# Score tiles as views of one three-bank PSUM tile, channel-major values, and a summed first projection, in a two-layer hybrid block

## The chip, the cores and the metric

The kernel runs on one core of one Trainium2 chip. The metric is the device time of one execution in microseconds (us); lower is better. PE is TensorE, DVE VectorE, ACT ScalarE, POOL GpSimd, SP SyncE; PSUM has eight banks of 512 fp32 columns on each of its 128 partitions.

## The reference

Two layers act on 512 image tokens and 256 context tokens of width 1024. Cut to what matters here:

```
for i in range(2):
    u = modulate(rmsnorm(h, norm1_g[i]), sh1, sc1) @ w_in[i]      # and the same for the context
    y_a = ssd_mixer(...);  y_b = diff_mixer(...);  y_c = gqa_mixer(...);  y_d = mla_mixer(...)
    h = h + g1 * (concat(y_a, y_b, y_c, y_d) @ w_out[i])
    h = h + g2 * (relu(modulate(rmsnorm(h, norm2_g[i]), sh2, sc2) @ mlp_w1[i])**2 @ mlp_w2[i])
return rmsnorm(h, final_norm_g)
```

`y_b` is a differential attention (two softmaxes for each of 4 heads), `y_c` and `y_d` are ordinary attentions of 4 heads each, `y_a` is a chunked state-space scan. Image queries attend to the 768 keys of image and context, context queries (layer 0 only) to the 256 context keys.

## The kernel before, in words

Activations lie channel-major, 8 tiles of 128 channels by 768 tokens (`XS` the 512 of the image, `CS` the 256 of the context). Every fp32 product is made from fp32r parts: a weight and an activation are each split in a high and a low part (`split`, L699), and three matmuls (high by high, high by low, low by high) are summed for each tile of the contraction (`gemm`, L726). One matmul has 512 columns for the image, and its partner 256 for the context.

`big_gemm` (L736) makes one output tile of 128 channels by 768 tokens (layer 1, which needs only the image: 512 or 256 tokens) in one PSUM tile from `ps_s` (L487), 48 matmuls in all, then hands it to an `evac`: in the MLP's first half ACT's relu (`up_jobs`, L1678, names `r<-p` in the profile), in its second half and in the output projection DVE's residual sums (`residual`, L1613, `h<-p`, `h<-pq`, `h<-pr`). `scores` (L1043) uses the same kind of PSUM tile for the 128 x 768 scores of one head and one block of queries; DVE takes their maximum (`maxed`, `d_m<-d_s`) and ACT their exponential (`exped`, `d_p<-d_s,d_m`). The probabilities are normalised, transposed on PE (`g_t<-ident,g_p`) and multiplied with the values. All other products, transposes and sums use PSUM tiles of one bank (`ps_t`, `ps_g`, ..., tag "g").

PSUM before: two tiles of 1024 columns (tag "S", two banks each) and four single banks.

The values of the differential attention and of the second attention (`dv`, `gv`) are made token-major by `v_start` and `v_step` (L872, L880): for each of 6 blocks of 128 tokens and each of 8 contraction tiles three matmuls of 384 columns. In layer 0 they are the first product: it runs contraction tile by contraction tile while the tiles `xn_0` to `xn_7` of the first norm become ready. `pdk` (first keys) follows.

The order of the work is not the order of the code. Every call on an engine is recorded by `Plan.take` (L217) with a cost from a small model; `Plan.order` (L245) then simulates the five engines and writes each engine's instructions in the order in which that simulation starts them; `Plan.issue` (L322) emits them in this one global order. All instructions of the profile therefore stand at the helper's line L331. The framework below adds the waits: it keeps a record for each PSUM or SBUF tile of who wrote and who read it last, in the order of emission. `Later` stands for a tile before its buffer is known.

Of the kernel before, what the change touches and what calls it, by code (L numbers as in the profile page):

```python
# [19 lines left out]
P = 128  # L20
# [17 lines left out]
def _r(c, n=P):  # L38
# [10 lines left out]
    "ckv": _r(C_CKV),  # L49
}  # L50
T_COLS = np.concatenate([_r(C_DV, 256), _r(C_GV)])
# [67 lines left out]
class Later:  # L119


    def __init__(self, pool, shape, dt, name, tag, bufs):
        self.args = (pool, shape, dt, name, tag, bufs)
        self.dt, self.tag, self.bufs = dt, tag, bufs
        self.made = None
        self.reads, self.writes = [], []
        self.left, self.end, self.first, self.last, self.kind, self.slot = 0, 0.0, None, None, None, None
        self.cols = int(np.prod(shape[1:]))
        self.base = np.empty(shape, np.int8)
        self.mem = self.base.__array_interface__["data"][0]  # L130

    def ap(self):
        pool, shape, dt, name, tag, bufs = self.args
        if self.made is None and bufs == 1:
            self.made = pool.tile(list(shape), dt, name=name, tag=tag, bufs=1)
# [15 lines left out]
class Pool:  # L151
# [3 lines left out]
    def tile(self, shape, dt, name, tag, bufs):  # L155
        t = Later(self.pool, shape, dt, name, tag, bufs)
        return View(t, (), t.base)


class Op:  # L160


    def __init__(self, n, eng):
        self.n, self.eng, self.calls, self.cost, self.late = n, eng, [], 0.0, 0.0
        self.before, self.after, self.tiles = set(), [], []
        self.start = self.end = 0.0


class Plan:
# [15 lines left out]
    def cost(self, eng, name, args, kw, out):  # L185
# [3 lines left out]
        if eng == "PE":  # L189
# [5 lines left out]
            m = w.width()  # L195
# [19 lines left out]
        return 0.45, 1.2  # L215

    def take(self, eng, fn, name, args, kw):  # L217
        out = kw["out"] if "out" in kw else args[0]
        writes = [x for x in (out, kw.get("accum_out")) if isinstance(x, View)]
# [8 lines left out]
        op.calls.append((fn, args, kw))  # L228
        op.cost += cost
# [15 lines left out]
    def order(self):  # L245
        tags = {}
        for op in self.ops:
            op.wait = len(op.before)
            op.rank = op.n - (self.EARLY if op.eng not in ("PE", "SP") and any(t.tag in ("S", "g") for t in op.tiles) else 0)
# [9 lines left out]
        ready = {e: [] for e in free}  # L259
        held = []  # L260
# [25 lines left out]
        while len(out) < len(self.ops):  # L286
            best = None
            for e, ops in ready.items():
                if not ops:
                    continue  # L290
# [6 lines left out]
            op = min((o for o in ready[e] if o.at <= s), key=lambda o: o.rank)  # L297
            ready[e].remove(op)
            cost = op.cost
# [6 lines left out]
            if e == "SP":  # L306
                dma = max(dma, op.end) + op.bytes / 250e3
# [14 lines left out]
    def issue(self):  # L322
        import os
        out = self.order()
        if os.environ.get("PLAN"):
            report(out)
# [47 lines left out]

def report(out):
    free, idle = {}, {}
    for op in out:
        e = op.eng
        w = int(op.start // 50)
        g = op.start - free.get(e, 0.0)  # L380
        idle.setdefault(e, {}).setdefault(w, 0.0)
        idle[e][w] += g
        free[e] = op.start + op.cost
    print("plan ends", max(o.end for o in out), {e: round(sum(o.cost for o in out if o.eng == e), 1) for e in free})
    for e in ("PE", "DVE", "ACT"):
        print(e, [round(idle[e].get(w, 0.0), 1) for w in range(40)])
# [46 lines left out]
def hybrid_block_kernel(ctx: ExitStack, tc: tile.TileContext, a: dict, out: bass.AP, dbg=None):  # L433
# [18 lines left out]
    NSC = 2  # L452
    GAP = 8
    UP_MODS = (1, 2, 3, 4)
    DN_MODS = ((1, 1, 2, 1, 2, 1, 2, 1), (1, 1, 2, 1, 2, 1, 2, 1), (1, 1, 2, 1, 2, 1, 2, 1), (2, 2, 2, 2, 2, 2, 2, 2))
    ORD0 = "gk ga gb cqx z0 xs0 xs1 cq0 b c z1 ckv".split()
    ORD1 = "gk ga gb z0 b xs1 cqx xs0 z1 c cq0 ckv".split()
# [28 lines left out]

    def ps_s(name):  # L487
        return pp.tile([P, 1024], F32, name=name, tag="S", bufs=2)

    def ps_t(name):  # L490
        return pp.tile([P, 512], F32, name=name, tag="g", bufs=4)

    def ps_v(name):
        return pp.tile([P, 512], F32, name=name, tag="g", bufs=4)

    def ps_o(name):
        return pp.tile([P, 512], F32, name=name, tag="g", bufs=4)

    def ps_g(name):
        return pp.tile([P, 512], F32, name=name, tag="g", bufs=4)  # L500

    def ps_r(name):
        return pp.tile([P, 512], F32, name=name, tag="g", bufs=4)
# [335 lines left out]
    def v_weights(l, q):  # L839
        return weights(f"wv{l}_{q}", a["wv"][l, :, q], 384, gtt if l == 0 else tt)  # L840

    wv = [v_weights(0, q) for q in range(4)]
    for i in range(3):
        mod_dma(i)
        next(wv[i])
# [9 lines left out]
    xn = [pair(f"xn0_{k}") for k in range(KT)]  # L855
    def xn_start(i):
# [10 lines left out]
        for k, t in late:  # L867
            for si, s in ((0, XS), (1, CS)):
                (LO0 if si in LOP else stt)(out=xn[k][1][:, s], in0=t[:, s], scalar=sh[:, k, si : si + 1], in1=f(xn[k][0][:, s]),
                    op0=ALU.add, op1=ALU.subtract)  # L870

    def v_start(l):  # L872

        lay[l].dv = [unit(f"dv{l}_{i}", (P, 3, 256)) for i in range(2)]
        lay[l].gv = unit(f"gv{l}", (P, 6, P))
        big = [ps_s(f"pv{l}_{i}") for i in range(2)]
        return [big[0][:, 0:384], big[0][:, 512:896], big[1][:, 0:384], big[1][:, 512:896],
                ps_t(f"pva{l}")[:, 0:384], ps_t(f"pvb{l}")[:, 0:384]]

    def v_step(l, vps, w, xn, k):  # L880
        for t in range(6):
            for wi, xi in ((0, 0), (1, 0), (0, 1)):
                mm(vps[t], xn[k][xi][:, P * t : P * t + P], w[k % 2][wi],
                   start=k == 0 and wi == 0 and xi == 0, stop=k == KT - 1 and xi == 1)
            yield 0.49
        if k == KT - 1:
            for t in range(6):
                act(lay[l].dv[t // 3][:, t % 3], vps[t][:, 0:256], AF.Copy)
                nc.vector.tensor_copy(lay[l].gv[:, t], vps[t][:, 256:384])

    def value_of(gen):
        while True:
            try:
                next(gen)
            except StopIteration as e:
                return e.value

    for i, s in enumerate((XS, CS)):
        run(rstd_of(f"n1_0_q{i}", psq[i], rb, s))
    ws = [value_of(wv[0])]  # L900
    mod_done(0, mod_load(0))
    xn_start(0)
    ws.append(value_of(wv[1]))
    m = mod_load(1)
    mod_dma(3)
    next(wv[3])
    vps = v_start(0)
    for q in range(4):
        run(v_step(0, vps, ws[q], xn, 2 * q))
        if q < 3:  # L910
            mod_done(q + 1, m)
            xn_start(q + 1)
        if q < 2:
            ws.append(value_of(wv[q + 2]))
        run(v_step(0, vps, ws[q], xn, 2 * q + 1))
        if q < 2:
            m = mod_load(q + 2)
# [58 lines left out]
    def mixers(l, xn, yd, h, ys):  # L976
# [7 lines left out]
        raw = {}  # L984
        done = set()
# [13 lines left out]
        def proj(name, toks, evac, how, after=None):  # L999
            def use(w):  # L1000
                yield from how(f"p{name}{l}", w, xn, toks, evac, len(TILES[name]))
# [4 lines left out]
        def v_jobs():  # L1006
            vps = []

            def use(w, q):
                if q == 0:  # L1010
                    flush()
                    vps.extend(v_start(l))
                for k in (2 * q, 2 * q + 1):
                    yield from v_step(l, vps, w, xn, k)

            return [(lambda q=q: v_weights(l, q), lambda w, q=q: use(w, q)) for q in range(4)]
# [26 lines left out]
        def scores(name, passes, t):  # L1043
# [68 lines left out]
        def diff_attn(j):  # L1112
# [24 lines left out]
            def vcols(hh, kt):  # L1137
                return L.dv[kt // 3][:, kt % 3, 64 * (2 * j + hh) : 64 * (2 * j + hh) + 64]
# [16 lines left out]
        def plain_attn(name, j, jobs, vcols, kout, flag, s_cost):  # L1155
            while flag not in done:
# [258 lines left out]
        def silu_z(name):  # L1415
            def evac(ps, s):
                if name not in raw:
                    raw[name] = unit(f"sz{name}{l}")
                t = sc(f"zt{name}{l}_{s.start}", s.stop - s.start)
                ts(t, ps, -80.0, None, op0=ALU.max)  # L1420
                sigmoid_of(t)
                tt(out=raw[name][:, s], in0=ps, in1=t, op=ALU.mult)
# [102 lines left out]
        def ready(j):  # L1525
            if ("dk", j, 1, 1) in dst and ("dq", j, 1, 1) in dst:
                done.add(("d", j))

        def dproj(n, how):
            toks = BOTH if n[:2] == "dk" else QT  # L1530

            def after():
                yield from diff_prep(n[:2], int(n[2]))
                yield K.hop_d
                ready(int(n[2]))

            return proj(n, toks, keep(n, 1.0 if n[:2] == "dk" else 32.0 ** -0.5), how, after)
# [9 lines left out]
        def gproj(n, how=side_gemm):  # L1547
            toks = BOTH if n in ("cqx", "b", "xs0", "xs1", "gk", "ckv") else QT
# [4 lines left out]
                     "c": setter("ssd"), "z1": setter("z"), "ckv": setter("mla")}.get(n)  # L1553
# [284 lines left out]
```

## Time and profile before

| | us |
|---|---|
| median of 3 runs (lowest to highest) | 1814.16 (1813.57 to 1814.26) |
| the profiled execution's own time | 1812.9 |
| its span in the profile | 1811.2 |
| PE busy in the span | 1732.4 |
| DVE, ACT, POOL busy | 1085.0, 875.6, 469.4 |

The profile shows one execution. Busy time is the time in which an engine has an instruction in work; "idle before" in a group is the time in which the engine had nothing before an instruction of that group, and the arrow names what ended it. PEclk is the share of full speed that was granted to TensorE. A name as `p<-a_0h,w_0s` is output from inputs; the digits of layers and buffers are left out. In time, layer 0's mixers and attention take some 25 to 425 us, its output projection and MLP 425 to 1075, layer 1's mixers 1075 to 1475, and its output projection and MLP the rest.

### The profile page before, as it was taken

To read this page: it belongs to the slowest core of one execution; us is meant where nothing else is said; L and a number is where in the kernel's file an instruction comes from. 1 tells how busy PE (TensorE), PEld (TensorE's weight loads), DVE (VectorE), ACT (ScalarE), POOL (GpSimd) and SP (SyncE) were. 2 spreads that over 40 slices of the span, in tenths; PEclk is the share of its full clock that TensorE was granted. 3 is DMA by queue.
4 is the path that set the end of the run, shared out by engine and by line. 5 is a ranking of instruction groups with operands and counts; after the bars stand their busy time and mean duration, and the time that the engine had idled before them with its cause. 6 is when DMAs were issued, how large, how long until landed. Compare 5 with 4: busy or idle time off the path is not lost. (4 is left out here: it accounts for less than half of the span.)

```text
span 1811.2 us, 30203 instructions
## 1 busy us (share of the span) xinstructions
PE 1732.4 (96%) x11206; PEld 1464.8 (81%) x11206; DVE 1085.0 (60%) x2112; ACT 875.6 (48%) x1776; POOL 469.4 (26%) x437
## 2 busy tenths in 40 slices
PE   6999999899999999999999999999799999999997
PEld 4878787677878888888888888887678998888886
DVE  4476968787584864543544184887886873333324
ACT  4355767687455223123122353777676762323243
POOL 2322342120244002001002664335110320101056
PEclk9999999999999999999999999999899999999999
DMA  9375431024344543432433334422014552323333
GB/s 354 94 214 150 122 105 37 17 53 162 109 157 141 171 141 96 158 118 87 156 123 99 133 107 133 127 77 59 12 49 152 172 177 93 97 95 94 97 110 126
DMA packets 117330, 216.28 MB, mean 119 GB/s; under 512 B 15424, under 2 KB 24640, under 8 KB 117184
## 3 DMA queue, kind: packets, MB, share of 16 engines
q1 hardware_dynamic: 117184, 214.36, 38.1%
q8 instruction: 88, 1.44, 0.3%
q14 instruction: 58, 0.48, 0.1%
HBM read 185.99 MB, written 8.13 MB: 107 GB/s over the span
## 5 line engine op out<-in xcount | busy, mean ns | idle before, releaser
L331 ACT ACTIVATE w_0s<-w 128x512 fp32r<-128x512 f32 x256 | 160.9, 630 | 387.4 <-PE p L331 352.2
L331 POOL TENSOR_TENSOR r<-r 128x512 f32<-128x512 f32 (+2 forms) x80 | 92.5, 1156 | 652.1 <-ACT a_0h L331 387.4
L331 DVE TENSOR_TENSOR w_0s<-w,w_0s 128x512 fp32r<-128x512 f32 x216 | 149.9, 697 | 184.2 <-ACT w_0s L331 179.1
L331 DVE SCALAR_TENSOR_TENSOR h<-p,modT,h 128x512 f32<-128x512 f32 (+1 forms) x104 | 63.0, 625 | 140.4 <-PE p L331 140.4
L331 ACT ACTIVATE r<-p 128x512 f32<-128x512 f32 (+2 forms) x80 | 47.8, 597 | 166.6 <-PE p L331 165.2
L331 DVE SCALAR_TENSOR_TENSOR junk<-mv,cb 128x512 bf16<-128x512 f32 x128 | 90.2, 716 | 46.2 <-DMA mv<-in_modw_dram 45.4
L331 DVE TENSOR_REDUCE d_m<-d_s 128x1 f32<-128x768 f32 (+1 forms) x80 | 66.4, 846 | 34.8 <-PE d_s L331 33.9
L331 ACT ACTIVATE d_p<-d_s,d_m 128x768 f32<-128x768 f32 (+1 forms) x80 | 65.0, 816 | 37.0 <-DVE d_m L331 28.0
L331 POOL TENSOR_TENSOR w_0s<-w,w_0s 128x512 fp32r<-128x512 f32 x40 | 54.2, 1363 | 28.1 <-ACT w_0s L331 26.3
L331 POOL TENSOR_TENSOR acc<-acc,sq 128x256 f32<-128x256 f32 (+1 forms) x48 | 49.9, 1041 | 42.3 <-ACT sq L331 41.8
L331 PE MATMUL p<-xm_0h,w_0s 128*128 128x512 f32 (+1 forms) x176 | 54.7, 357 | 0.1
L331 PE MATMUL p<-xm_3h,w_0s 128*128 128x512 f32 (+1 forms) x176 | 54.5, 356 | 0.0
L331 PE MATMUL p<-a_0h,w_0s 128*128 128x512 f32 (+1 forms) x176 | 54.1, 354 | 0.3 <-POOL w_0s L331 0.2
L331 PE MATMUL p<-xm_7h,w_0s 128*128 128x512 f32 (+1 forms) x176 | 54.2, 354 | 0.0
L331 PE MATMUL p<-xm_4h,w_0s 128*128 128x512 f32 (+1 forms) x176 | 54.0, 353 | 0.0
L331 PE MATMUL p<-a_5h,w_0s 128*128 128x512 f32 (+1 forms) x176 | 54.0, 353 | 0.0
L331 PE MATMUL p<-a_3h,w_0s 128*128 128x512 f32 (+1 forms) x176 | 54.0, 353 | 0.0
L331 PE MATMUL p<-xm_6h,w_0s 128*128 128x512 f32 (+1 forms) x176 | 53.9, 353 | 0.0
L331 PE MATMUL p<-a_7h,w_0s 128*128 128x512 f32 (+1 forms) x176 | 53.8, 352 | 0.0
L331 PE MATMUL p<-xm_5h,w_0s 128*128 128x512 f32 (+1 forms) x176 | 53.8, 352 | 0.0
L331 PE MATMUL p<-xm_2h,w_0s 128*128 128x512 f32 (+1 forms) x176 | 53.8, 352 | 0.0
L331 PE MATMUL p<-a_4h,w_0s 128*128 128x512 f32 (+1 forms) x176 | 53.8, 352 | 0.0
(2346 smaller groups left out, 5552.6 us busy)
## 6 DMA issues: line engine op xcount, KB each, us to landing
w<-in_w_dram SPq DMA_DIRECT2D x320, 256.0 KB, 2.6
mv<-in_modw_dram SPq DMA_DIRECT2D x96, 256.0 KB, 2.7
mk<-in_modk_dram SPq DMA_DIRECT2D x64, 256.0 KB, 3.4
wr<-in_wout_dram SPq DMA_DIRECT2D x32, 256.0 KB, 2.7
h<-in_xT_dram SPq DMA_DIRECT2D x16, 384.0 KB, 7.6
mw<-in_mod_dram SPq DMA_DIRECT2D x16, 384.0 KB, 6.3
wo<-in_wout_dram SPq DMA_DIRECT2D x32, 192.0 KB, 2.4
wv<-in_wv_dram SPq DMA_DIRECT2D x16, 192.0 KB, 5.0
```

The source lines that it names most:

```text
L331: i = fn(*[x.real() if isinstance(x, View) else x for x in args], **{k: x.real() if isinstance(x, View) else x for k, x in kw.items()}).ins
```

## The change

1. `ps_s` no longer gives two tiles of two banks each. One tile `wide` of 1536 columns (three banks) is made once, and the two slots S0 and S1 are views of its columns 0 to 767 and 768 to 1535. Each slot has one bank of its own and half of the middle one. Since a matmul stays in one bank, `big_gemm` and `scores` cut slot S0 at column 512 and S1 at column 256. For views (`of`) no buffer dependency is added by hand.
2. The bank that becomes free goes to the general tiles: five instead of four.
3. The planner gets a rule (`barred`): a sum may not be opened in a shared bank while another slot has one open there.
4. `dv` and `gv` become ordinary channel-major projections (`dv0`, `dv1`, `gvv`) and are transposed on PE afterwards (`v_prep`: 18 transposes and 6 ACT copies for each layer, in place of 144 matmuls' token-major form and 12 copies).
5. In layer 0 four projections (`dk0`, `dq0`, `dv0`, `dk1`) are summed side by side, contraction tile by contraction tile, as the norm tiles come (`first_step`), where the values stood before.
6. The planner's model of DMAs changes (latency 1.2 to 1.4, 250 to 330 KB/us), and `silu_z` copies its PSUM tile to SBUF first.

The diff, cut to its core:

```diff
+    wide = pp.tile([P, 2 * NT], F32, name="wide", tag="wide", bufs=1)
+    turn = [0]
     def ps_s(name):
-        return pp.tile([P, 1024], F32, name=name, tag="S", bufs=2)
+        i = turn[0] = 1 - turn[0]
+        return pp.tile([P, NT], F32, name=name, tag=f"S{i}", bufs=1, of=(wide, NT * i)), 256 if i else 512
     def ps_t(name):
-        return pp.tile([P, 512], F32, name=name, tag="g", bufs=4)
+        return pp.tile([P, 512], F32, name=name, tag="g", bufs=NG)
...
# Later.ap
+        if self.made is None and self.of is not None:
+            self.made = self.of[0].t.ap()[:, self.of[1] : self.of[1] + self.cols]
...
# Plan.order
+        def barred(op):
+            return any(begins and any(t not in ts for t in opened.get(b, ())) for b, (begins, _, ts) in op.sums.items())
...
# Plan.issue
-                            if t.last is not None:
+                            if t.last is not None and t.of is None:
...
# big_gemm
-        ps = ps_s(name)
-        b = toks[0].start
-        yield from gemm([(ps[0:m, t.start - b : t.stop - b], t) for t in toks], w, xs)
-        evac(ps[0:m, 0 : toks[-1].stop - b], slice(b, toks[-1].stop))
+        ps, cut = ps_s(name)
+        b, e = toks[0].start, toks[-1].stop
+        if e - b == NT:
+            at = [(0, cut), (cut, NT)]
+        else:
+            at = [(cut % 512, cut % 512 + e - b)]
+        yield from gemm([(ps[0:m, c0:c1], slice(b + c0 - at[0][0], b + c1 - at[0][0])) for c0, c1 in at], w, xs)
+        evac(ps[0:m, at[0][0] : at[-1][1]], slice(b, e))
...
# scores
-            u.ps = ps_s(f"{name}_s")
-            cuts = [(0, 512), (512, 768)] if u.n == NT else [(0, 256)]
-            for i, (q, k) in enumerate(passes):
-                for b, e_ in cuts:
+            u.ps, cut = ps_s(f"{name}_s")
+            cuts = [(0, cut), (cut, NT)] if u.n == NT else [(0, 256)]
+            for b, e_ in cuts if cut == 256 else cuts[::-1]:
+                for i, (q, k) in enumerate(passes):
...
# layer 0's start
+    FIRST = ("dk0", "dq0", "dv0", "dk1")
+    def first_step(k):
+        for n in FIRST:
+            w = fw[n, k // 4]
+            c = slice(P * (k % 4), P * (k % 4) + P)
+            for wi, xi in ((0, 0), (0, 1), (1, 0)):
+                for i, (o, t) in enumerate(first[n]):
...
+    for i in range(4):
+        first_step(2 * i)
+        if i < 3:
+            mod_done(i + 1, m)
+            xn_start(i + 1)
+        first_step(2 * i + 1)
...
+        def v_prep(name, n):
+            L.v_[name] = unit(f"t{name}{l}")
+            for i in range(2):
+                ps = ps_t(f"tv{name}{l}_{i}")
+                for t in range(3):
+                    nc.tensor.transpose(ps[:, P * t : P * t + P], raw[name][:, P * (3 * i + t) : P * (3 * i + t) + P], ident)
+                act(L.v_[name][:, 384 * i : 384 * i + 384], ps[:, 0:384], AF.Copy)
+                yield 0.33
```

The built programs show what this does to the instructions and their waits. First PE in layer 0's MLP, at the step from one output tile of the second half (`w20_2_1`) to the next (`w20_2_2`). Before, the two tiles are separate:

```order
L331 MATMUL p20_2_1_0_9169<-a0_2_7h_9107,w20_2_1_0s1_9105 128x512
L331 MATMUL p20_2_1_0_9169<-a0_2_7h_9107,w20_2_1_0s1_9105 128x256
L331 MATMUL p20_2_2_0_9242<-a0_2_0h_8609,w20_2_2_0s0_9142 128x512 [waits DVE_49,Activation_49]
L331 MATMUL p20_2_2_0_9242<-a0_2_0h_8609,w20_2_2_0s0_9142 128x256
L331 MATMUL p20_2_2_0_9242<-a0_2_0l_8637,w20_2_2_0s0_9142 128x512
```

With the change both are `wide`:

```order
L350 MATMUL wide_133<-a0_2_7h_8969,w20_2_1_0s1_8967 128x512
L350 MATMUL wide_133<-a0_2_7h_8969,w20_2_1_0s1_8967 128x256
L350 MATMUL wide_133<-a0_2_0h_8478,w20_2_2_0s0_9004 128x256 [waits Activation_49]
L350 MATMUL wide_133<-a0_2_0h_8478,w20_2_2_0s0_9004 128x512
L350 MATMUL wide_133<-a0_2_0l_8506,w20_2_2_0s0_9004 128x256
L350 MATMUL wide_133<-a0_2_0l_8506,w20_2_2_0s0_9004 128x512
L350 MATMUL wide_133<-a0_2_0h_8478,w20_2_2_0s0_9004 128x256
L350 MATMUL wide_133<-a0_2_0h_8478,w20_2_2_0s0_9004 128x512 [waits DVE_49]
L350 MATMUL wide_133<-a0_2_1h_8552,w20_2_2_0s0_9004 128x256
```

The first matmul of the new tile waits for its weight (ACT) and, before, also for an older reader of its buffer. With the change the sixth matmul waits for DVE, and the twelfth (three pairs on) once more: followed through the semaphores' values, these are the two residual sums that read the tile just finished. On DVE they stand so:

```order
L350 SCALAR_TENSOR_TENSOR h1_1_4882<-wide_133,modT_303,h1_1_4882 128x512 [waits PE_49]
L350 SCALAR_TENSOR_TENSOR h1_1_4882<-wide_133,modT_303,h1_1_4882 128x256 [waits PE_49]
```

Before, the first of the two waits for the last matmul of its own tile, and the second for nothing. With the change the first waits for the fifth matmul of the next tile (the one ahead of PE's waiting one) and the second for the eleventh. The first reads columns 0 to 511 of `wide`; the matmul that waits for it writes columns 1024 to 1535.

Then DVE at layer 0's first scores. Before, each maximum waits for its own scores on PE:

```order
L331 TENSOR_REDUCE d0_0_0_0_0_m_1003<-d0_0_0_0_0_s_995 128x1 [waits PE_49]
L331 TENSOR_REDUCE d0_0_0_0_1_m_1015<-d0_0_0_0_1_s_1005 128x1 [waits PE_49]
```

With the change the second and later ones wait for ACT, which is the exponential of the other slot:

```order
L350 TENSOR_REDUCE d0_0_0_0_0_m_968<-wide_133 128x1 [waits PE_49]
L350 TENSOR_REDUCE d0_0_0_0_1_m_989<-wide_133 128x1 [waits Activation_49]
L350 RECIPROCAL d0_0_0_0_0_m_968<-d0_0_0_0_0_m_968 128x1
L350 TENSOR_SCALAR d0_0_0_0_0_p_984<-d0_0_0_0_0_p_984,d0_0_0_0_0_m_968 128x768 [waits DMAHW3_49,DVE_49]
L350 TENSOR_REDUCE d0_0_0_1_0_m_1008<-wide_133 128x1 [waits Activation_49]
```

## Rows read from the trace of the kernel before

**Rows 1.** The page: busy time, share of the span and instructions of each engine.
```profile
PE 1732.4 (96%) x11206; PEld 1464.8 (81%) x11206; DVE 1085.0 (60%) x2112; ACT 875.6 (48%) x1776; POOL 469.4 (26%) x437
```

**Rows 2.** Busy time by stage: stretch, its length, engines (instructions), PEclk, DMA share, GB/s.
```profile
25.00:75.00 50.00, 45.71 (x314) 39.24 (x315) 21.67 (x43) 18.01 (x36) 12.82 (x11) 0.90 0.60 208
75.00:425.00 350.00, 326.69 (x2596) 263.83 (x2594) 267.46 (x570) 233.12 (x532) 95.32 (x93) 0.98 0.38 107
425.00:1075.00 650.00, 644.01 (x3835) 555.27 (x3833) 350.99 (x669) 223.52 (x395) 156.61 (x118) 1.00 0.40 128
1075.00:1475.00 400.00, 382.06 (x2797) 330.45 (x2797) 308.86 (x609) 273.22 (x587) 120.78 (x117) 0.98 0.35 103
1475.00:1750.00 275.00, 275.00 (x1230) 225.23 (x1229) 100.54 (x150) 90.57 (x157) 31.49 (x31) 1.00 0.31 99
```

**Rows 3.** Timeline of PE in layer 0's MLP, from one output tile to the next: start, length.
```profile
903.24 0.51 PE L331 MATMUL p<-a_7h,w_0s 128*128 128x512 f32 x2
903.59 0.51 PE L331 MATMUL p<-a_0h,w_0s 128*128 128x512 f32 x2
```

**Rows 4.** Timeline of DVE at the same place; in brackets the idle time before.
```profile
903.79 1.14 DVE L331 SCALAR_TENSOR_TENSOR h<-p,modT,h 128x512 f32<-128x512 f32 x2 [2.30 <-PE p L331]
```

**Rows 5.** Groups by shape that read `big_gemm`'s tiles: busy, mean ns, idle before them.
```profile
L331 DVE SCALAR_TENSOR_TENSOR h<-p,modT,h 128x512 f32<-128x512 f32 x56 | 42.1, 751 | 113.3 <-PE p L331 113.3
L331 DVE SCALAR_TENSOR_TENSOR h<-p,modT,h 128x256 f32<-128x256 f32 x48 | 22.9, 478 | 27.1 <-PE p L331 27.1
L331 ACT ACTIVATE r<-p 128x768 f32<-128x768 f32 x24 | 19.5, 812 | 86.9 <-PE p L331 86.9
L331 ACT ACTIVATE r<-p 128x512 f32<-128x512 f32 x32 | 19.1, 598 | 65.9 <-PE p L331 65.9
L331 ACT ACTIVATE r<-p 128x256 f32<-128x256 f32 x24 | 9.2, 382 | 13.7 <-PE p L331 12.3 <-POOL r L331 0.8 <-DVE n_r L331 0.2
```

**Rows 6.** DVE and ACT reading one PSUM tile in turns, around 67.3 us (timeline).
```profile
67.27 0.29 DVE L331 COPY gv<-pv 128x128 f32<-128x128 f32 x1 [4.29 <-PE pv L331]
67.59 0.39 ACT L331 ACTIVATE dv<-pv 128x256 f32<-128x256 f32 x1 [0.69 <-DVE gv L331]
```

**Rows 7.** Groups by shape that read the score tiles of the differential attention.
```profile
L331 DVE TENSOR_REDUCE d_m<-d_s 128x1 f32<-128x768 f32 x64 | 60.2, 953 | 22.0 <-PE d_s L331 21.3
L331 ACT ACTIVATE d_p<-d_s,d_m 128x768 f32<-128x768 f32 x64 | 57.5, 902 | 28.3 <-DVE d_m L331 21.7 <-DVE d_p L331 2.8 <-PE d_t L331 2.2
```

**Rows 8.** Timelines of DVE and ACT: two score tiles read at one time.
```profile
136.56 0.96 DVE L331 TENSOR_REDUCE d_m<-d_s 128x1 f32<-128x768 f32 x1 [0.22 <-PE d_s L331]
...
136.80 0.90 ACT L331 ACTIVATE d_p<-d_s,d_m 128x768 f32<-128x768 f32 x1
```

**Rows 9.** Timelines of layer 0's start: first norm tile, first and last products of the values, first keys.
```profile
24.98 1.12 ACT L331 ACTIVATE xn_0h<-n_t,modT 128x512 fp32r<-128x512 f32 x2 [3.03 <-DVE n_t L331]
25.75 1.01 PE L331 MATMUL pv<-wv_0s,xn_0h 128*128 128x384 f32 x2 [2.11 <-ACT xn_0h L331]
...
68.28 0.33 PE L331 MATMUL pva<-wv_3s,xn_7h 128*128 128x384 f32 x1
68.45 0.33 PE L331 MATMUL pva<-wv_3s,xn_7l 128*128 128x384 f32 x1
...
69.15 0.51 PE L331 MATMUL pdk<-xn_0h,wdk00s 128*128 128x512 f32 x2
...
77.52 0.39 PE L331 MATMUL pdq<-xn_0h,wdq00s 128*128 128x512 f32 x1
```

**Rows 10.** What PE waited for between 75 and 125 us: total, times, longest.
```profile
PE d_s L331 <- DMA sdq<-hldq_0l: 4.0, 2, 2.3
```

**Rows 11.** The group of PE's 128 x 128 transposes of one attention.
```profile
L331 PE MATMUL g_t<-ident,g_p 128*128 128x128 f32 x208 | 34.8, 301 | 10.2 <-DVE g_p L331 7.8 <-DVE mk_1l L331 1.3 <-DVE ee L331 0.6
```

**Rows 12.** Short stretches of 25 us by busy time and granted clock (columns as in rows 2).
```profile
300.00:325.00 25.00, 21.52 (x190) 16.50 (x192) 22.00 (x58) 18.19 (x45) 3.13 (x3) 1.00 0.16 49
1275.00:1300.00 25.00, 20.61 (x157) 16.32 (x157) 19.74 (x52) 13.67 (x29) 3.97 (x4) 0.81 0.03 12
```

More of the change, by code (lines that the diff above doesn't have):

```diff
@@ L165, in __init__ @@
         self.before, self.after, self.tiles = set(), [], []
+        self.sums = {}
         self.start = self.end = 0.0
@@ L214, in cost @@
         self.bytes = 4 * (x.box[1] - x.box[0]) * x.width()
-        return 0.45, 1.2
+        return 0.45, 1.4
     def take(self, eng, fn, name, args, kw):
+        behind, parts = kw.pop("behind", None), kw.pop("parts", ())
         out = kw["out"] if "out" in kw else args[0]
-        writes = [x for x in (out, kw.get("accum_out")) if isinstance(x, View)]
+        writes = [x for x in (out, kw.get("accum_out"), *parts) if isinstance(x, View)]
         reads = [x for x in list(args) + list(kw.values()) if isinstance(x, View) and all(x is not y for y in writes)]
@@ L228, in take @@
         op.calls.append((fn, args, kw))
+        if behind is not None:
+            op.before |= {o for _, o in behind.t.writes if o is not op}
+        if eng == "PE":
+            for v in writes:
+                if v.t.of is not None:
+                    wide, c0 = v.t.of
+                    for b in range((c0 + v.box[2]) // 512, (c0 + v.box[3] - 1) // 512 + 1):
+                        x = op.sums.setdefault((wide.t, b), [False, False, []])
+                        x[0], x[1] = x[0] or kw.get("start", True), not kw.get("stop", True)
+                        if v.t not in x[2]:
+                            x[2].append(v.t)
         op.cost += cost
@@ L248, in order @@
             op.wait = len(op.before)
-            op.rank = op.n - (self.EARLY if op.eng not in ("PE", "SP") and any(t.tag in ("S", "g") for t in op.tiles) else 0)
+            op.rank = op.n - (self.EARLY if op.eng not in ("PE", "SP") and any(t.tag in ("S0", "S1", "g") for t in op.tiles) else 0)
             for o in op.before:
@@ L288, in order @@
             for e, ops in ready.items():
+                if e == "PE":
+                    ops = [o for o in ops if not o.sums or not barred(o)]
                 if not ops:
@@ L296, in order @@
             s, e = best
-            op = min((o for o in ready[e] if o.at <= s), key=lambda o: o.rank)
+            op = min((o for o in ready[e] if o.at <= s and not (o.sums and barred(o))), key=lambda o: o.rank)
             ready[e].remove(op)
+            for b, (_, stays, ts) in op.sums.items():
+                (opened.setdefault(b, set()).update if stays else opened.setdefault(b, set()).difference_update)(ts)
             cost = op.cost
@@ L372, in __getattr__ @@
         return lambda *args, **kw: self.plan.take(self.eng, fn, name, args, kw)
[L375 to L386, printed above, removed]
 class Weave:
@@ L836, in sigmoid_of, with first_load, first_split @@
         act(t, t, AF.Exp, scale=-1.0)
[L839 to L845, printed above, removed]
+    FIRST = ("dk0", "dq0", "dv0", "dk1")
+    LAST = {"dq0": "dk0", "dk1": "dv0"}
+    fw = {}
+    def first_load(i):
+        for n in FIRST:
+            fw[n, i] = sb.tile([P, 512], F32, name=f"w{n}0_{i}", tag="wr", bufs=NWR)
+            ld(fw[n, i], a["win"][0, :, T_OFF[n] + 512 * i : T_OFF[n] + 512 * i + 512])
+    def first_split(i):
+        for n in FIRST:
+            x = sb.tile([P, 2, 512], F32R, name=f"w{n}0s{i}", tag="ws", bufs=NWS)
+            split(x[:, 0], x[:, 1], fw[n, i], gtt)
+            fw[n, i] = x
+    mod_dma(0)
+    first_load(0)
+    mod_dma(1)
+    mod_dma(2)
     psq = [ps_t(f"n1_0_ms{i}")[:, 0 : s.stop - s.start] for i, s in enumerate((XS, CS))]
@@ L855, in hybrid_block_kernel @@
     xn = [pair(f"xn0_{k}") for k in range(KT)]
+    first_split(0)
+    for i, s in enumerate((XS, CS)):
+        run(rstd_of(f"n1_0_q{i}", psq[i], rb, s))
     def xn_start(i):
@@ L880, in v_step @@
[L880 to L901, printed above, removed]
+    first = {}
+    def first_tiles():
+        for n in FIRST[0:2]:
+            ps, cut = ps_s(f"p{n}0")
+            at = ((0, 512), (512, NT)) if cut == 512 else ((256, NT), (0, 256))
+            first[n] = [(ps[:, c0:c1], s) for (c0, c1), s in zip(at, (XS, CS))]
+        both = ps_t("pfirst")
+        for i, n in enumerate(FIRST[2:4]):
+            first[n] = [(ps_t(f"p{n}0"), XS), (both[:, 256 * i : 256 * i + 256], CS)]
+        nil = sil[:, 0, 2:3].to_broadcast([P, 512])
+        mm(both, ident, nil, start=True, stop=False)
+        mm(wide[:, 512:1024], ident, nil, start=True, stop=False, parts=[first[n][1][0] for n in FIRST[0:2]])
@@ new lines, in first_step @@
+    def first_step(k):
+        for n in FIRST:
+            w = fw[n, k // 4]
+            c = slice(P * (k % 4), P * (k % 4) + P)
+            for wi, xi in ((0, 0), (0, 1), (1, 0)):
+                for i, (o, t) in enumerate(first[n]):
+                    begins = k == 0 and wi == 0 and xi == 0
+                    ends = k == KT - 1 and wi == 1
+                    mm(o, w[:, wi, c], xn[k][xi][:, t], start=begins and i == 0, stop=ends and (i == 0 or n in LAST),
+                       parts=[first[LAST[n]][1][0]] if ends and i == 1 and n in LAST else ())
@@ L902, in hybrid_block_kernel @@
+    m = mod_load(0)
+    mod_done(0, m)
     xn_start(0)
-    ws.append(value_of(wv[1]))
     m = mod_load(1)
     mod_dma(3)
[L906 to L917, printed above, removed]
+    first_load(1)
@@ L1155, in plain_attn @@
         def plain_attn(name, j, jobs, vcols, kout, flag, s_cost):
-            while flag not in done:
+            while flag not in done or "gv" not in done:
                 yield None
```

107 lines of the change are left out of this document (55 added, 52 removed).

## The prediction, made before the result was known

> **What bounds the kernel now.** I read the page's busy times first: PE is busy for 1732.4 us [rows 1] of a span of 1811.2, so all its idle time is 78.8 us. The other engines are far from full. Then the stages [rows 2]: in the stretch from 425 to 1075 us, layer 0's output projection and MLP, PE is idle for 650 - 644.0 = 6 us, and in layer 1's from 1475 to 1750 us for none. In the two mixer stages it is idle for 23.3 and 17.9 us, and DVE is 76% busy there. In the first 50 us of the norm and the values it is idle for 4.3 us, at a mean granted clock of 0.90, a mix of TensorE's two levels of 1.2 and 2.4 GHz (0.5 and 1.0). So the kernel is bound by PE, and whatever stops PE in an MLP lengthens the run by as much. The detail that matters is how PE passes from one output tile to the next. Its pairs of matmuls start every 0.35 us across the boundary between two tiles [rows 3]. DVE's residual sum of the finished tile starts 0.20 us after PE began the next tile [rows 4] and reads while PE works in the other buffer. The readers of these tiles wait for PE, never the other way: DVE was idle for 113.3 / 56 = 2.0 us ahead of each first residual sum and ACT for 3.6 us ahead of each relu [rows 5].
>
> **The change: the MLPs and the output projection.** Both buffers become views of one tile, and the program after shows what that does to the waits: a reader of one view waits for the last matmul emitted ahead of it in either, and the next matmul in either view waits for that reader, whichever bank it writes. PE then stands still from the end of the matmul that the reader waits for to the end of the read. I followed the semaphores of all readers of `wide` in these stages: 196 have no matmul between the one that they wait for and the one that waits for them. They are 62 residual sums of 512 columns and 62 of 256, 24 relus of 768, 26 of 512 and 22 of 256. With the means of [rows 5] the reads alone last 62 x 0.751 + 62 x 0.478 + 24 x 0.812 + 26 x 0.598 + 22 x 0.382 = 46.6 + 29.6 + 19.5 + 15.5 + 8.4 = 119.6 us. To each comes the way from PE to the reader, 0.20 us as in [rows 4], and back. For the way back the nearest row is one engine released by another over one PSUM tile: DVE's copy ends at 67.27 + 0.29 = 67.56, ACT's starts at 67.59 [rows 6], 0.03 us. I take 0.25 us for both: 196 x 0.25 = 49. **Term 1: +169 us** (95 in layer 0, 73 in layer 1); lower bound 120, if the ways cost nothing. Nothing covers this: behind the waiting matmul stand only further matmuls of the same queue. ACT and DVE have room, since they waited for PE here anyway.
>
> **The change: attention.** There 112 matmuls wait for a maximum or an exponential of `wide`, and 52 maxima wait for the other slot's exponential. Before, two such reads overlapped: a maximum of 0.96 us from 136.56 and an exponential of 0.90 us from 136.80 [rows 8]. Other matmuls often stand between, so a wait need not cost its full time. Laid along the new order with the means of [rows 7] (0.953 and 0.902 us) and 0.25 us for the ways, 53 of the 112 waits have less PE work ahead of them than the read takes; what is missing sums to 37 us. Some of it takes the place of the 41 us that PE idles there already; a DVE at 76% will be late for some more. **Term 2: +40 us**, with 10 as the lower bound (only the largest gaps remain) and 100 as the upper (most of the 112 at nearly 0.95 us).
>
> At this point a rule speaks against the change. Reads of two score tiles by DVE and ACT at one time, and PE writing beside them, cost nothing in [rows 8, 4], where each tile has its own banks. The Trainium skill ("PSUM — Partial Sum Buffer", section "PSUM bank collisions raise a hardware error") says that engines must be kept apart by bank, two readers included, whatever the columns. By it alone only the reads that touch the middle bank would have to be fenced; what that gives is the second rival.
>
> **The change: values and start.** A channel-major projection takes 8.4 us (77.52 - 69.15 [rows 9]); three take 25.1 us. The token-major form is 144 matmuls at 68.45 - 68.28 = 0.17 us [rows 9], 25 us. So that exchange is even, and what is added is 18 transposes for each layer at 34.8 / 208 = 0.17 us [rows 11], 36 in all. The 6 copies that they need replace 12 smaller ones on engines that are not full. **Term 3: +6 us** at most; I take 4, since DVE and ACT lose a few reads and the upper end is a mean with waits in it.
>
> At the start PE works on the values from 25.75 to 69.15 us [rows 9]: 43.4 us for 25 us of matmuls (some at a lower clock), paced by the norm tiles. The change puts four projections there, 4 x 8.4 = 33.5 us. So 8.5 us more of PE's work lie in the same stretch, if the norm tiles come as before. The keys and queries of the first head pair are also ready sooner, and 4.0 us of waits for the stacked queries [rows 10] may go. Against it, the first weights are 4 loads of 256 KB, and a late one shifts everything; the opening matmuls of the shared banks are two. **Term 4: -9 us**, between 0 (the norm tiles come later by as much) and -12.5 (both gains in full). The fifth general bank and the planner's constants show in no wait that I can price: PE never waits for a general bank for long in these rows, so I cost them at nothing; what covers them is PE's own queue.
>
> **Sum.** 1812.9 (the profiled execution) + 169 + 40 + 4 - 9 = 2016.9 us. The profiled execution lies 1.3 us under the median of 1814.16, which is less than the terms are known to. Forecast **2017 us**.
>
> **Rivals.**
> 1. *The waits cost nothing and only the start remains: faster.* If every read had ended by the time PE reaches the matmul that waits for it, terms 1 and 2 would vanish: 1812.9 + 4 - 9 = 1808, 0.3% faster. The point from which this decides is a read that ends before PE arrives. For it: in attention half the waits have enough work ahead. Against it: in the MLPs the read cannot start before the matmul just ahead of PE's waiting one has ended, and lasts 0.38 to 0.81 us [rows 5]. Chance 0.05.
> 2. *Only the middle bank is fenced.* Then the reads from a slot's own bank would not stop PE. Left are 24 relus of 768 at 1.06 us and 24 residual sums (half of 512, half of 256 columns, 1.00 and 0.73 us): 25 + 21 = 46 us instead of 169, which gives 1894 us. Against it: the program's waits also stand on layer 1's 512-column tiles, each in a bank of its own. Chance 0.06.
> 3. *The clock falls with the gaps.* A 25 us stretch of layer 1's mixers in which PE was idle for 4.4 us had a granted clock of 0.81, a mix of both levels; one of layer 0's with 3.5 us idle kept 1.00, the upper level [rows 12]. In the MLPs PE would stand for 1.7 us after each 8.4 us. At 0.86 over the 919 us of PE work in the two MLP stretches of [rows 2] the price would be 919 x 0.16 = 150 us: 2167. Against it: these gaps are near 1 us each and evenly spread, and layer 0's attention kept 0.98 with 23 us of idle time. Chance 0.07.
> 4. *The waits double in attention.* The chain maximum, exponential, next maximum is serial over both slots now; if DVE and ACT cannot keep it up, term 2 goes to 100 or beyond: 2077 and more. Inside my range up to 2095; beyond it 0.04.
>
> **How the numbers follow.** My forecast with its bounds has 0.78. Its low end is the reads alone with the smallest attention term and the full start: 1812.9 + 120 + 10 - 12.5 = 1930. Its high end is 1812.9 + 169 + 100 + 6 = 2088, rounded up to 2095 for ways longer than 0.25 us. The range is therefore 1930 to 2095; the rivals 1 to 3 and the rest of 4 lie outside. A difference under 0.2% (3.6 us) could not be told from no change. Slower by more: 0.78 + 0.06 + 0.07 + 0.04 = 0.95. Rival 1 gives 6 us of gain and holds 0.05; of it 0.04 go to faster and 0.01 to no difference.
>
> **What the profile after would show.** Right: PE idle near 285 us instead of 79, with its busy time changed by a few us; PE's waits led by the residual sums (124 times, near 107 us) and the relus (72 times, near 61 us); the stage of layer 0's output projection and MLP longer by about 95 us; in the timeline a PE gap of about 1.0 us five matmuls into each tile of the second MLP half. Also a maximum and an exponential of `wide` never at one time. The four first projections should end near 70 us. Wrong: PE pairs every 0.35 us across the boundary as before, or a total under 1900. If the gaps are there and the total is right but attention is not longer, term 2 was mis-sized.

## The result, and the profile after

The changed kernel takes 2072.1 us (2071.8 to 2075.5), against 1814.2 us for the kernel before on the same chip: 1.143 times as long, 95% interval 1.141 to 1.145, or 258 us more. The forecast was 2017 (1930 to 2095).

The page of the profile after, busy time of each engine, span 2070.3 us (to hold against [rows 1]):

```profile
PE 1808.7 (87%) x11246; PEld 1463.1 (71%) x11246; DVE 1088.7 (53%) x2092; ACT 884.1 (43%) x1791; POOL 466.4 (23%) x441
```

PE is now idle for 2070.3 - 1808.7 = 262 us instead of 79, and its busy time has grown by 76 us with nearly the same number of matmuls. The busy times of the other engines moved by less than 9 us.

What PE waited for in the profile after, the longest in total (total, times, longest):

```profile
PE wide L350 <- DVE h L350: 91.9, 123, 1.7
PE wide L350 <- ACT r L350: 53.9, 76, 1.0
PE wide L350 <- ACT m_p L350: 12.7, 10, 5.8
PE wide L350 <- ACT d_p L350: 11.9, 15, 2.6
PE wide L350 <- DVE m_m L350: 11.3, 15, 2.1
```

The readers of `wide` lead: residual sums and relus in the MLPs, exponentials and maxima in the attentions. In the waits of before none of them came to more than 4 us.

To see where the time went I cut both traces at the same events: first scores, first product of the second output projection (whose weights are `wq`), and layer 1's first product of `xn_0`. Before (columns as in [rows 2]: stretch, length, PE, PEld, DVE, ACT, POOL, PEclk, DMA, GB/s), in the order layer 0's mixers, its output projection and MLP, layer 1's mixers, its output projection and MLP:

```profile
102.70:476.60 373.90, 352.88 (x2762) 284.45 (x2763) 283.02 (x607) 252.26 (x579) 86.49 (x87) 0.98 0.36 104
476.60:1067.90 591.30, 586.63 (x3482) 509.75 (x3481) 315.12 (x607) 192.67 (x325) 149.58 (x114) 1.00 0.41 131
1067.90:1404.80 336.90, 318.43 (x2251) 266.18 (x2250) 254.25 (x504) 225.11 (x482) 99.12 (x93) 0.98 0.31 87
1404.80:1811.20 406.40, 391.10 (x2170) 337.60 (x2168) 185.99 (x301) 166.66 (x317) 103.20 (x99) 0.99 0.37 118
```

The same four stages after:

```profile
97.90:503.10 405.20, 369.36 (x2807) 292.57 (x2808) 277.62 (x603) 254.38 (x587) 83.07 (x86) 0.96 0.34 99
503.10:1202.20 699.10, 612.58 (x3482) 507.96 (x3481) 314.81 (x608) 193.76 (x328) 145.83 (x115) 1.00 0.35 111
1202.20:1579.40 377.20, 331.94 (x2268) 267.11 (x2267) 257.62 (x488) 228.18 (x486) 103.18 (x98) 0.96 0.28 76
1579.40:2070.30 490.90, 414.66 (x2170) 337.08 (x2168) 184.51 (x301) 167.41 (x317) 100.45 (x99) 0.99 0.31 97
```

The MLP stages grow by 107.8 and 84.5, 192.3 us in sum, with exactly the same number of matmuls (3482 and 2170) and the same granted clock. The mixers grow by 31.3 and 40.3, 71.6 us. The start up to the first scores gains 4.8 us. Together this is the 259.1 us by which the span grew.

One step from tile to tile shows the mechanism. I call a standstill of PE behind a reader of `wide` a stop. Timeline of PE after, at a boundary in the second half of layer 0's MLP (start, length, in brackets the idle time before):

```profile
1008.52 0.51 PE L350 MATMUL wide<-a_0h,w_0s 128*128 128x512 f32 x2
1008.87 0.51 PE L350 MATMUL wide<-a_0l,w_0s 128*128 128x512 f32 x2
1009.22 0.39 PE L350 MATMUL wide<-a_0h,w_0s 128*128 128x512 f32 x1
1010.45 0.39 PE L350 MATMUL wide<-a_0h,w_0s 128*128 128x256 f32 x1 [0.84 <-DVE h L350]
1010.68 0.51 PE L350 MATMUL wide<-a_1h,w_0s 128*128 128x512 f32 x2
```

And of DVE and of PE's weight loads there:

```profile
1009.65 0.75 DVE L350 SCALAR_TENSOR_TENSOR h<-wide,modT,h 128x512 f32<-128x512 f32 x1 [2.74 <-PE wide L350]
...
1009.10 0.19 PEld L350 LDWEIGHTS wide<-a_0h,w_0s 128*128 128x128 f32 x1
1010.45 0.19 PEld L350 LDWEIGHTS wide<-a_0h,w_0s 128*128 128x128 f32 x1 [1.16 <-DVE h L350]
```

PE makes five matmuls of the new tile, as the order said, and stands. The pair that began at 1009.22 would have had its second matmul at 1009.45 (a 512-column matmul takes 0.23 us in an undisturbed row of pairs every 0.35, the other 0.12). DVE starts 0.20 us after that point, reads for 0.75 us to 1010.40, and PE starts at 1010.45: 1.00 us lost, as predicted. But the next pair begins at 1010.68, 0.23 us after a matmul that needs 0.12. These further 0.11 us go with the weight load: in flow it runs ahead of its matmul (1009.10 for 1009.22), behind the wait it starts together with it. This is no single case: in the two MLP stages of this trace 211 matmuls start over 0.25 us later than the flow has it (23 before), and the matmul behind such a one is late by 0.107 us in the median. So one stop costs its read and 0.36 us, not 0.25. That also explains the larger busy time in the MLP stages (49.5 of the 76 us): the profile models a matmul's end, and a lone one is shown with 0.39 us.

That the guard is by tile and not by bank is seen in layer 1, where 256-column tiles lie in the banks that the views do not share. PE stops in the fourth contraction tile of a new sum, until ACT's relu of the finished tile has ended:

```profile
1643.09 0.38 ACT L350 ACTIVATE r<-wide 128x256 f32<-128x256 f32 x1 [0.71 <-PE wide L350]
...
1643.52 0.39 PE L350 MATMUL wide<-xm_3h,w_0s 128*128 128x256 f32 x1 [0.52 <-ACT r L350]
```

The rule of the Trainium skill ("PSUM — Partial Sum Buffer", section "PSUM bank collisions raise a hardware error") asks for a guard by bank; these stops are more than that rule needs, and they come from the record of one tile. No run here tests the rule itself. Over the whole trace, no matmul into `wide` starts inside a read of `wide`, and no maximum overlaps an exponential of it; before, such reads of score tiles overlapped for 28.0 us in all.

### The profile page after: what moved, and what is told of

It is laid out like the page before. It is cut to its first block, busy times and chain, and to the rows that moved or that the text cites. A ratio compares the mean times of both kernels' runs of the same rounds, so it can differ in the third digit from the quotient of the medians.

```text
span 2070.3 us, 30167 instructions
## 1 busy us (share of the span) xinstructions
PE 1808.7 (87%) x11246; PEld 1463.1 (71%) x11246; DVE 1088.7 (53%) x2092; ACT 884.1 (43%) x1791; POOL 466.4 (23%) x441
## 5 line engine op out<-in xcount | busy, mean ns | idle before, releaser
L350 DVE SCALAR_TENSOR_TENSOR h<-wide,modT,h 128x256 f32<-128x256 f32 (+1 forms) x136 | 82.4, 609 | 267.8 <-PE wide L350 267.6
L350 PE MATMUL wide<-a_1h,w_0s 128*128 128x512 f32 (+1 forms) x176 | 63.2, 386 | 38.5 <-DVE h L350 35.6
L350 ACT ACTIVATE d_p<-wide,d_m 128x768 f32<-128x768 f32 (+1 forms) x80 | 64.8, 813 | 71.7 <-DVE d_m L350 53.5
L350 DVE TENSOR_REDUCE d_m<-wide 128x1 f32<-128x768 f32 (+1 forms) x80 | 65.7, 847 | 54.3 <-PE wide L350 38.6
L350 PE MATMUL wide<-xm_0h,w_0s 128*128 128x512 f32 (+1 forms) x176 | 61.3, 373 | 23.8 <-ACT r L350 20.6
L350 PE MATMUL wide<-a_0h,w_0s 128*128 128x512 f32 (+1 forms) x176 | 60.1, 368 | 18.9 <-DVE h L350 16.5
L350 PE MATMUL wide<-xm_1h,w_0s 128*128 128x512 f32 (+1 forms) x176 | 57.5, 370 | 21.2 <-ACT r L350 16.4
L350 PE MATMUL wide<-xm_3h,w_0s 128*128 128x512 f32 (+1 forms) x176 | 55.0, 357 | 4.3 <-ACT r L350 3.7
L350 PE MATMUL wide<-a_3h,w_0s 128*128 128x512 f32 (+1 forms) x176 | 54.7, 356 | 3.1 <-DVE h L350 2.3
L350 PE MATMUL wide<-a_5h,w_0s 128*128 128x512 f32 (+1 forms) x176 | 54.1, 354 | 0.8 <-DVE h L350 0.8
```

## The experiments

**Two tiles again.** Everything of the change stays but the shared tile and, with its three banks, the fifth general bank and one opening matmul:

```diff
-    wide = pp.tile([P, 2 * NT], F32, name="wide", tag="wide", bufs=1)
...
-        return pp.tile([P, NT], F32, name=name, tag=f"S{i}", bufs=1, of=(wide, NT * i)), 256 if i else 512
+        return pp.tile([P, 1024], F32, name=name, tag="S", bufs=2), 512
...
-    NG = 5
+    NG = 4
...
```

> The changed kernel with one thing undone: score and product tiles are again two PSUM tiles of their own (1024 columns, two banks each, four general banks). Channel-major values, the summed first projections and the planner's constants stay. Theory (the waits over one shared tile are the whole loss): both MLPs and both mixer stages come back to their lengths of before, the start keeps its gain of about 5 us, the 36 transposes cost at most 6: 1805 to 1820 us. Rival (the new order, the values' new form or the planner's constants carry part of the 72 us that the mixer stages lost): the MLPs come back, the mixers do not, 1830 to 1885 us.

Measured: 1828.5 us (1824.2 to 1833.3), 1.007 times the kernel before (1.006 to 1.009). So taking the shared tile out gives back 2072.1 - 1828.5 = 244 of the 258 us. The time lies between the two expectations: the theory is right in the main, but 14 us stay. The profiled execution of this kernel, the slowest of its four (span 1831.5, 20.3 us longer than before), begins its first scores 3.1 us earlier than before (99.6 for 102.7) and has layer 0's MLP back (590.7 for 591.3). The mixers, from first scores to `wq`, are 10.7 and 8.9 us longer than before, and layer 1's MLP stage 4.4:

```profile
99.60:484.20 384.60, 360.02 (x2824) 287.23 (x2825) 280.42 (x603) 255.56 (x587) 82.90 (x86) 0.97 0.36 107
1074.90:1420.70 345.80, 323.90 (x2269) 266.81 (x2268) 261.84 (x490) 229.91 (x488) 104.32 (x99) 0.96 0.30 84
1420.70:1831.50 410.80, 393.46 (x2170) 338.98 (x2168) 188.80 (x301) 166.64 (x317) 103.17 (x99) 0.99 0.37 116
```

**The MLPs in tiles of their own.** Only the scores share `wide`; `big_gemm` sums in two general banks:

```diff
-        ps, cut = ps_s(name)
...
+        outs = [(ps_g(f"{name}_{t.start}")[0:m, 0 : t.stop - t.start], t) for t in toks]
+        yield from gemm(outs, w, xs)
+        for o, t in outs:
+            evac(o, t)
...
```

> The changed kernel with one part undone in another way: products of the MLP and the output projection are summed in pairs of general banks (one of 512, one of 256 columns, each a tile of its own); only the scores still share one tile. Theory: the MLP and output stages lose their stops, 192 us by the stage times, and the mixers keep theirs: 1870 to 1890 us. Rival (the shared tile slows the MLPs by something else, such as weights that come late in the new order): over 1920 us.

Measured: 1881.4 us (1880.2 to 1882.6). The MLPs' part of the loss is 2072.1 - 1881.4 = 191 us, and what the sharing costs the mixers is 1881.4 - 1828.5 = 53 us. Its MLP stages are those of before, to about a microsecond:

```profile
504.10:1094.30 590.20, 585.69 (x3482) 509.26 (x3482) 327.09 (x631) 195.98 (x373) 162.08 (x138) 1.00 0.42 131
1474.10:1880.90 406.80, 391.51 (x2170) 337.57 (x2168) 185.72 (x301) 166.15 (x317) 103.85 (x99) 0.99 0.38 118
```

**One read instead of two.** In the changed kernel:

```diff
                 def evac(ps, s):
+                    if len(ss) > 1:
+                        x = sm(f"dn{l}_{g}_{k}")
+                        act(x, ps, AF.Copy)
+                        ps = x
                     for i, t in enumerate(ss):
```

> The changed kernel, but in layer 0 the 24 tiles of the MLP's second half that have 768 columns are copied out by one read of ACT (128x768) into SBUF, and the two residual sums read the copy. The number of stops falls by 24, one ACT read of 0.81 us stands in place of two DVE reads of 0.75 and 0.48. Theory (every stop costs its read and 0.34 us besides: the way there, the way back and the first matmul's later start): 24 x (1.23 + 0.68 - 0.81 - 0.34) = 18 us less, 2050 to 2058 us. Rival (only the read's own time counts): 24 x 0.42 = 10 us less, 2060 to 2064. Rival (the ACT copy is late behind other work): no gain, 2070 or more.

Measured: 2053.8 us (2052.2 to 2055.4), 18.4 us less than the changed kernel: the price of a stop has a fixed part, of about the expected size. Layer 0's output projection and MLP, the stage with the edit, is 699.1 - 681.1 = 18.0 us shorter:

```profile
504.00:1185.10 681.10, 606.22 (x3481) 508.06 (x3480) 314.51 (x608) 210.46 (x352) 145.51 (x115) 1.00 0.36 114
```

This is the shortest test of the fixed part, since the kernel does more work (24 copies of 768 columns) and is faster.

**The shared tile alone.** The kernel before, with the shared tile, the cuts, five general banks and the planner's rule; of the values' six sums two lie in the views and four in general banks:

```diff
...
-        return pp.tile([P, 1024], F32, name=name, tag="S", bufs=2)
+        return pp.tile([P, NT], F32, name=name, tag=f"S{i}", bufs=1, of=(wide, NT * i)), 256 if i else 512
...
+        big = [ps[:, 0:384] if cut == 512 else ps[:, 384:768] for ps, cut in big]
+        return big + [ps_t(f"pv{x}{l}")[:, 0:384] for x in "abcd"]
```

> The kernel before with the first part of the change alone: the shared three-bank tile, five general banks, the planner's rule for shared banks. Values, start and planner's DMA constants are those of before; the first values' six sums lie in the two views' own banks and four general ones. Theory (the shared tile's stops cost 191 us in the MLPs and 53 in the mixers, whatever else is changed): 1814 + 244 = 2058, 2045 to 2070 us. Rival (the mixers' part depends on the order that the other edits bring): under 2040 or over 2075.

Measured: 2072.9 us (2071.8 to 2074.1), at 1.142 (1.140 to 1.145) the same as the whole change, and 3 us above the expected stretch. Put in alone, the shared tile thus costs 2072.9 - 1815.4 = 257.5 us; taken out of the whole change it gave back 244. So its cost depends on the other edits by some 14 us. Its MLPs lose 193 us by the same cuts, as they should. Its mixers lose 69.5:

```profile
101.10:508.40 407.30, 365.97 (x2762) 287.63 (x2763) 279.61 (x607) 251.52 (x579) 87.26 (x87) 0.95 0.33 96
1210.40:1583.40 373.00, 333.44 (x2250) 272.11 (x2249) 253.21 (x502) 225.38 (x480) 97.35 (x92) 0.94 0.28 78
```

So the mixers' part is 53 us on the order of the change and about 70 on the order of before. The MLPs' part comes out alike in both orders (191 and 193); the mixers' part does not. A likely reason is which matmuls happen to lie between a score's reader and the next score, but no run shows it, and the granted clock in the mixers is also a little lower here (0.95 and 0.94, where the run with the MLPs in tiles of their own has 0.96 in both).

**The start.** The run with two tiles, without the side-by-side sums:

```diff
...
-                jobs = [dproj(n) for n in ("dq1", "dv1")]
+                jobs = [dproj(n) for n in ("dk0", "dq0", "dv0", "dk1", "dq1", "dv1")]
...
-        first_step(2 * i)
...
-        first_step(2 * i + 1)
...
```

> The run with two tiles, without the four side-by-side sums at the start: layer 0's projections are all ordinary ones, one after the other, and begin on the norm tiles as they come. Theory (the side-by-side sums hide 33.5 us of products behind the norm tiles): only the first projection's image part, 5.6 us, is hidden, so some 28 us are lost: 1850 to 1862 us. Rival (the start is bound by loads and norm, and later stages have slack): less than 12 us lost, under 1840.

Measured: 1829.1 us (1828.8 to 1829.3): nothing is lost, beyond the scatter; the rival's time holds. The traces show where it goes. With the side-by-side sums (the run with two tiles), at 25 to 50, 75 to 100 and 100 to 125 us:

```profile
25.00:50.00 25.00, 23.51 (x166) 17.57 (x167) 12.16 (x24) 6.85 (x12) 2.21 (x3) 0.88 0.80 303
...
75.00:100.00 25.00, 19.12 (x131) 15.58 (x130) 15.40 (x15) 8.49 (x16) 15.12 (x10) 0.98 0.51 128
100.00:125.00 25.00, 15.94 (x88) 10.71 (x88) 16.32 (x29) 10.12 (x22) 0.00 (x0) 0.77 0.71 178
```

Without them:

```profile
25.00:50.00 25.00, 17.35 (x111) 10.16 (x112) 16.51 (x29) 9.90 (x17) 5.57 (x4) 0.66 0.81 304
...
75.00:100.00 25.00, 21.55 (x148) 16.90 (x147) 15.14 (x27) 11.92 (x26) 6.06 (x4) 0.93 0.65 187
100.00:125.00 25.00, 24.60 (x204) 20.66 (x205) 20.42 (x37) 14.57 (x31) 8.28 (x5) 1.00 0.63 161
```

Without the sums PE stands for 7.7 us at 25 to 50, at a granted clock of 0.66 (a mix of both levels). With them it is busy there, but it stands for 14.9 us at 75 to 125 and has 0.77 of the clock in the last stretch. Side by side, the sums of the first head pair's keys and queries end at 70.1 and 71.1 us, and the first scores begin at 99.6; one after the other they end at 54.8 and 64.7, and the first scores begin at 80.4. The queries' sum makes up 6.4 of these 19.2 us; how the rest arises in the chain from sums to scores was not followed. By the first product of the second output projection the two runs are level again, at 484.2 and 484.7 us. So what was hidden at the start was paid back before layer 0's mixers end.

**The planner's constants and the values' place.** Three smaller runs.

```diff
# two tiles, old DMA model
-        return 0.45, 1.4
+        return 0.45, 1.2
...
-                dma = max(dma, op.end) + op.bytes / 330e3
+                dma = max(dma, op.end) + op.bytes / 250e3
```

> The run with two tiles, and besides the planner's DMA constants of before (latency 1.2, 250 KB/us). Theory (the 14 us that the run with two tiles lies above the kernel before come from an order planned with DMAs that are too fast, so that stacked queries and weights come late): 1812 to 1820 us. Rival (they come from the values' new form, whose transposes and copies stand in the mixer stages, and from the clock): within 4 us of 1828.5.

Measured: 1840.7 us (1837.4 to 1841.7). Both theory and rival miss: the old constants are 12 us worse here, with the new order that they bring.

```diff
# two tiles, gvv later (layer 1 likewise)
-    ORD0 = "gk ga gb gvv cqx z0 xs0 xs1 cq0 b c z1 ckv".split()
+    ORD0 = "gk ga gb cqx z0 xs0 gvv xs1 cq0 b c z1 ckv".split()
```

> The run with two tiles, with the second attention's values (gvv) three places later in the order of the supporting projections. Theory (the values stand ahead of work that the mixers' long chains wait for, where before they were made at the start in both layers): 1815 to 1824 us. Rival (PE is bound by the sum of its work and the place does not matter): within 4 us of 1828.5.

Measured: 1832.6 us (1830.9 to 1833.0); no gain, the theory falls. The rival's stretch, too, is missed by 0.1 us.

```diff
# two tiles, transposes twice
-                for t in range(3):
+                for t in (0, 1, 2, 0, 1, 2):
                     nc.tensor.transpose(ps[:, P * t : P * t + P], raw[name][...], ident)
```

> The run with two tiles, with each of the 36 transposes of the values issued twice (the output is the same). Theory (they stand on PE's path in the mixers and cost their own time of 0.11 to 0.17 us): 4 to 6 us more than 1828.5. Rival (they fall in PE's idle times of the mixers): within 2 us.

Measured: 1831.3 us (1828.8 to 1832.1), 2.8 us more than without, with ranges that overlap (1824.2 to 1833.3 without): between the two answers, and not decided. By the two intervals against the kernel before (1.0057 to 1.0090 and 1.0071 to 1.0105), the second set of transposes costs between nothing and, as an estimate, some 7 us.

**The new constants alone.** The kernel before with the two constants of the change:

```diff
-        return 0.45, 1.2
+        return 0.45, 1.4
...
-                dma = max(dma, op.end) + op.bytes / 250e3
+                dma = max(dma, op.end) + op.bytes / 330e3
```

> The kernel before with the planner's new DMA constants alone (latency 1.4, 330 KB/us). Theory (the new constants describe this chip's loads better; going back to the old ones cost 12 us in the run with two tiles): 1800 to 1808 us. Rival (each set of constants brings another order, and a given order gains or loses by chance): 1810 to 1830 us.

Measured: 1809.7 us (1807.9 to 1812.5) beside 1815.4 (1811.5 to 1818.2) for the kernel before on the same chip: 0.997 (0.996 to 0.9985). The point lies between the two expectations. It is a gain of some 5 us, small but outside its interval, and the only version here that beats both kernels. That the constants fit the chip's loads better is not shown by it: another order could do the same. Its first scores begin at 94.2 us instead of 102.7.

## Why the prediction was right, and where its terms were off

- **Direction and cause: right.** The shared tile makes 244 of the 258 us when it is taken out of the change (the run with two tiles), and 257.5 when it is put in alone; the fifth general bank went with it both times. The rivals of free waits (1808) and of a fence of the middle bank alone (1894) are excluded by the gaps in both layers' MLPs. The clock did not fall in the MLPs: 1.00 and 0.99, as before; in the mixers it went from 0.98 to 0.96.
- **What the range owes to luck.** 191 + 53 + 14 = 258 us were measured where the terms gave 169 + 40 + 4 - 9 = 204. The high end left term 1 only 7 us of room, and term 1 missed by 22. Terms 3 and 4 had 11 us of room and missed by 19, together with what was costed at nothing. The total stayed inside because the 60 us of room in term 2, meant for something else, took up these misses.
- **Term 1, +169 us: measured 191 to 193.** The count of 196 stops (199 waits in the profile) and the reads' lengths held. What was mis-sized is the 0.25 us for the ways: the first matmul behind a wait also pays for its own weight load, 0.11 us, which no row of before showed. 196 x 0.11 = 22 us, and 169 + 22 = 191. The 3.6 us for which ACT stood ahead of each relu held only for the 24 relus of 768 columns; ahead of those of 512 and 256 it was 65.9 / 32 = 2.1 and 13.7 / 24 = 0.6 us.
- **Term 2, +40 us: measured 53** by the pair of runs, within its bounds of 10 to 100. The same 0.11 us for each of 112 waits would be 12 us of it; that this is the whole difference was not tested. On the order of before the part is nearer 70.
- **Term 3, +4 us: open.** Doubling the transposes gave +2.8 us, inside the scatter; the values' new form itself was never taken back.
- **Term 4, -9 us: this step failed.** The four sums did end near 72 us, about where I put them, but I ended the reckoning there, as if work hidden at the start shortened the run by as much. The gain to the first scores is 4.8 us, and the run without the sums takes as long as the one with them: nothing of the gain is left at the end.
- **The rest, costed at nothing:** without the shared tile, terms 3 and 4 with everything else in the change come to +14 us instead of -5; with it, to -1 (2072.1 against 2072.9 for the shared tile alone). Most of it lies in the mixers of the run with two tiles, as a little more of each: in layer 1, 5.5 us more PE busy time, 3.4 us more idle time, a granted clock of 0.96 instead of 0.98. Which edit brings it is not settled: putting the old constants back or moving `gvv` did not remove it, and the transposes are, by the estimate above, at most some 7 us of it. Not tested are the values' new form as a whole, the copy in `silu_z`, the fifth general bank by itself (that PE never waits for such a bank for long stands in none of the rows), and a condition in the changed code (`ready`) by which a head pair's attention starts only when its values are done too.
- **Signs in the profile.** Predicted were 124 stops for residual sums and 72 for relus; there are 123 and 76. The predicted totals, 107 and 61 us, read 91.9 and 53.9 there, and PE's busy time grew by 76 us where I said a few; its idle time is 262 us, not 285: part of each stop is booked as a busy matmul. The starts of the matmuls, not the idle column, give the true price. The gap five matmuls into the tile, the stage 108 us longer (95 predicted) and the maxima and exponentials that never overlap came as said.

## What to carry to other kernels

Before two buffers become views of one allocation, ask at what grain the waits are kept: where a tile is the unit, two views are one buffer, and double buffering is gone although every byte is separate. Count the stops in the built program, and price each as read, ways and the weight load that no longer runs ahead. Work hidden at the start counts only if what waits next is ready sooner: here the sums made side by side were all finished late.

## What was not expected of the hardware

- A matmul that waits for a semaphore starts its weight load only when the wait ends: load and matmul both at 1010.45, and the next pair 0.11 us late (0.107 in the median over 211 such matmuls). In flow the load began 0.12 us ahead of its matmul. The Trainium skill ("PSUM — Partial Sum Buffer", section "Engine vs sequencer instructions") says that TensorE's queue lets a weight load overlap matmuls in flight; the flowing rows agree, and the stopped ones show where that ends.
- Gaps of about 1 us every few us did not lower the clock: in layer 0's MLP PE is idle for 699.1 - 612.6 = 86.5 us with a granted clock of 1.00, the upper level.
